# Zero-padded query blocks in one attention, and one PSUM copy with GpSimd adds in the other

## The chip, the core and the metric

The kernel runs on one core of a Trainium2 chip. A core has a matrix engine (TensorE, PE in the rows; its weight loads are listed apart as PEld), VectorE (DVE), ScalarE (ACT), GpSimd (POOL) and SyncE (SP), which issues most DMA transfers. The engines run side by side and wait for one another through semaphores; each takes its instructions in the order of the program. TensorE writes its results into PSUM, from where VectorE and ScalarE take them to SBUF. The metric is the time of one execution on the device, in microseconds (us); smaller is better.

## The reference

Two transformer blocks follow each other, on 1024 tokens of width 1024. Two of their stages matter here.

The first block has an attention with 8 heads of width 64, causal, with a forget gate `c`:

```python
s = jnp.einsum('bqhd,bkhd->bhqk', qb, k) * scale          # 128 queries a block
s = s + cqb[..., :, None] - c_bhs[..., None, :]
s = jnp.where(key_pos[None, :] <= q_pos[:, None], s, -jnp.inf)
p = jax.nn.softmax(s, axis=-1)
out = jnp.einsum('bhqk,bkhd->bqhd', p, v)
```

The second block has an attention with 16 query heads in 4 groups (4 heads share a key head), each block of 128 queries against its own, the previous and the next block of 128 keys and against 256 context keys, with a sink term in the softmax:

```python
s_lat = einsum('bqhgd,bshd->bhgqs', qb, kb) * scale       # up to 384 keys
s_ctx = einsum('bqhgd,bshd->bhgqs', qb, k_ctx) * scale    # 256 keys
p = softmax(concatenate([where(valid, s_lat, -1e30), s_ctx, sink]))
o = p_lat @ vb + p_ctx @ v_ctx
```

Around them stand projections, a gated unit, a feed-forward part, a convolution and a mixture of 16 experts; the change leaves these alone.

## The kernel before

Every fp32 number `x` that enters a matrix product is held as two fp32r numbers, a high part (a ScalarE copy) and a low part `x - high` (a VectorE subtraction), and a product is the sum of two or three products of parts. So PSUM results pass through both ScalarE and VectorE before TensorE uses them again.

**First attention.** The loop `for n in range(N + last + 1)` runs over 64 steps, a step being one head `h` and one block `i` of 128 queries, with `i + 1` blocks of 128 keys. `steps` interleaves the long blocks of a head (i = 7 to 4, score tile `sb` of two banks) with the short ones of the head before (i = 3 to 0, score tile `ss` of one bank), in pairs: two long, two short, and so on. Eight steps make one head's worth of work. Each of `sb` and `ss` has one buffer, so the scores of the second step of a pair wait until VectorE has read the first. The table `ORDB` gives the parts of a step and how many steps each lags behind: S, score products (lag 0); M, VectorE's masked minimum and addition, line 698 (0); E, ScalarE's exponential, line 706 (1); T, the transposition of the probabilities on TensorE, line 721 (3); H and L, high and low part, lines 727 and 731 (3 and 4); V, the product with the values, lines 740 and 741 (6); O, the output out of PSUM, lines 751 to 756 (6); F, the sums and final scale. Within a round the order on every engine is V, L, T, O, F, S, H, M, E.

The score product of 512 keys has two parts and, in the last chunk, the causal mask between them. `q` holds, for the head in question, high and low parts of the query stacked in 128 partitions, `k` the high part of the keys twice; that product (line 685) contracts over 128 partitions. The third product, high part of the query by the low part `l` of the keys, takes the 64 partitions `r` of the head alone (line 688); the other 64 partitions of `l` hold the low part of the other head of the pair.

**Second attention.** 32 units of a head group and a query block, four steps each, run through the table `ORD2` in the same manner, with lags up to 10 for the output (O) and 27 for the final scale (F). A unit takes four score products (lines 1411 to 1414, each over 128 partitions), four VectorE minima (line 1425), four exponentials (1432), five groups of transposes (1444), five high and low parts (1454, 1462) and ten products with the values (1474, 1475), which gather in one PSUM bank `po`, `[128, 512]`: partitions 0 to 63 are the part of the high, 64 to 127 that of the low value parts, columns are four heads by 128 queries. `po` has one buffer. `pv_out2` adds the two halves and puts heads 0 and 2 in partitions 0 to 63 of `og`, heads 1 and 3 in 64 to 127. In 28 of the 32 units (all but the last four) this takes four ScalarE copies out of PSUM (lines 1496 and 1497) and one GpSimd addition (1498). In most units `prep_k` or `prep_q` also stacks keys or queries of the next group, a chain of TensorE, ScalarE and VectorE.

Of the kernel before, what the change touches and what calls it, by code (L numbers as in the profile page):

```python
# [8 lines left out]
F32 = mybir.dt.float32  # L9
F32R = mybir.dt.float32r  # L10
# [3 lines left out]
AF = mybir.ActivationFunctionType  # L14
OP = mybir.AluOpType
# [3 lines left out]
P = 128  # L19
# [3 lines left out]
def fused(tc, x, mix_norm_g, w_in, b_f, sgu_ln_g, sgu_ln_b, w_s, b_s, out_norm_g, w_out,  # L23
# [13 lines left out]
    ACT, DVE, POOL, PE = nc.scalar, nc.vector, nc.gpsimd, nc.tensor  # L37
    act = nc.scalar.activation
    ES = ExitStack()
    L, R = "left", "right"  # L40

    def pool(es, name, bufs=1, side=L, space=None):
        kw = dict(name=name, bufs=bufs)
        if space is not None:
            kw["space"] = space
        else:
            kw["side"] = side
        return es.enter_context(tc.tile_pool(**kw))
# [4 lines left out]
    def rd(ap):  # L53
        return ap.bitcast(F32)

    def split(h, l, src, scale=None):
        if scale is None:
            act(h, src, AF.Copy)  # L58
            DVE.tensor_tensor(l, src, rd(h), op=OP.subtract)  # L59
        else:  # L60
            act(h, src, AF.Copy, scale=scale)
            DVE.scalar_tensor_tensor(l, src, scale, rd(h), op0=OP.mult, op1=OP.subtract)
# [101 lines left out]
    def wsrc(w, k0, kc, c0, n):  # L164
        return w[k0 * P:(k0 + kc) * P, c0:c0 + n].rearrange("(k p) n -> p k n", p=P)
# [151 lines left out]
    for src in (mix_norm_g, out_norm_g, ffn_norm_g, norm1_g_2, norm2_g_2, conv_w_2, b_mod_2, c_2, c_ctx_2):  # L317
        n = 1
# [166 lines left out]
    for g4 in range(2):  # L485
# [3 lines left out]
        o = slice(g4 * 4, g4 * 4 + 4)  # L489
# [84 lines left out]
    qk = []  # L574
# [60 lines left out]
    es_b = ExitStack()  # L635
# [4 lines left out]
    pst = pool(es_b, "pst", 4, space=PSUM)  # L640
    ps1 = pool(es_b, "ps1", 1, space=PSUM)
    pvs = pool(es_b, "pvs", 2, R)
    pol = pool(es_b, "pol", 3, R)
    psm = pool(es_b, "psm", 3, R)
    ppt = pool(es_b, "ppt", 2, R)
    ptn = pool(es_b, "ptn", 2, R)
# [5 lines left out]
    def prep(j):  # L652
        vs[j] = pvs.tile([P, NT, 2, P], F32R, name="vhl")
        h, l = vs[j][:, :, :, :64], vs[j][:, :, :, 64:]
        vv = vraw[:, :, j * P:(j + 1) * P].rearrange("p t (o d) -> p t o d", o=2)
        for o in range(2):
            if 2 * j + o not in cns:
                cn_load(2 * j + o)
        return [
            lambda: act(h, vv, AF.Copy),  # L660
            lambda: DVE.tensor_tensor(l, vv, rd(h), op=OP.subtract),
        ]

    steps = []
# [5 lines left out]
                steps += [(m, 7 - a), (m, 6 - a)]  # L670
    live, half, pts = {}, {}, {}

    def score_mm(n):
        h, i = steps[n]
        q, k, l = qk[h]
        r = slice(64 * (h % 2), 64 * (h % 2) + 64)
        nk = (i + 1) * P
        blk = slice(i * P, i * P + P)
        if i > 3:
            sp = psp.tile([P, T], F32, name="sb", bufs=1)  # L680
        else:
            sp = psp.tile([P, 512], F32, name="ss", bufs=1)
        for c0 in range(0, nk, 512):
            cs = slice(c0, min(c0 + 512, nk))
            PE.matmul(sp[:, cs], q[:, blk], k[:, cs], start=True, stop=False)  # L685
            if c0 + 512 >= nk:
                PE.matmul(sp[:, blk], idR, cmR, start=False, stop=False)
            PE.matmul(sp[:, cs], q[r, blk], l[r, cs], start=False, stop=True)  # L688
        live[n] = sp

    def score_max(n):
# [85 lines left out]
    def done(n, d):  # L777
        h, i = steps[n]
        if i == 0 and h % 2 and h < 7:
            for x, f in zip((FS[0], last + FS[1], last + FS[2], last + FS[3]),  # L780
                            (lambda j: pair_sum(j, 0), lambda j: pair_mul(j, 0), lambda j: pair_sum(j, 1), lambda j: pair_mul(j, 1))):
                if d == x:
                    f(h // 2)
        if (h, i) == (7, 0) and d == dict(ORDB)["E"] + 1:
            DVE.reciprocal(rinv, tns[3][:, 1].rearrange("p i o -> p (i o)"))
            rx[3] = sq.rearrange("p (i o d) -> p i (o d)", o=2, d=64)
            todo.append(lambda: DVE.tensor_copy(rx[3].rearrange("p i (o d) -> p (i o) d", o=2),
                                                rinv[:, :, None].to_broadcast([P, 16, 64])))
# [7 lines left out]
    def stage(f, n):  # L796
        if 0 <= n < N:
            f(n)

    ASQ = max(steps.index((5, 0)) + last + FS[3], steps.index((7, 7))) + 1  # L800
    table = dict(S=score_mm, M=score_max, E=score_exp, T=probs_T, H=probs_H, L=probs_L, V=even(pvmm), O=even(pv_out))
    for n in range(N + last + 1):
        if n < N and steps[n] in ((0, 7), (2, 7), (4, 7), (6, 7)):
            oT.append((pq if oT else po0).tile([P, T], F32, name="qk"))
        for c, d in ORDB:
            if c == "F":
                for d in range(last + 8):
                    stage(lambda m: done(m, d), n - d)
            else:
                stage(table[c], n - d)  # L810
        if n < N and steps[n][1] == 5 and steps[n][0] in (1, 3, 5):
            todo.extend(prep(steps[n][0] // 2 + 1))
        if n < N and steps[n] == (6, 7):

            r4, r5, rw, h4, l4, wh0, wl0 = [pq.tile([P, T], F32 if i < 3 else F32R, name="qk") for i in range(7)]
            k2 = lambda a: a[:, :768].rearrange("p (k n) -> p k n", k=2)
            nc.sync.dma_start(r4, d_sgu[0])
            nc.sync.dma_start(k2(rw), wsrc(w_out, 4, 2, 0, 384))
            nc.sync.dma_start(r5, d_sgu[1])
            todo.extend([lambda: split(h4, l4, r4), lambda: split(k2(wh0), k2(wl0), k2(rw))])  # L820
        if n < N and steps[n] == (7, 7):
            h5, l5, sqs, sq = [pq.tile([P, T], F32R if i < 2 else F32, name="qk") for i in range(4)]
            todo.append(lambda: split(h5, l5, r5))

            def attn_sq(j):
                act(sq if j else sqs, oT[j], AF.Square)
                if j:
                    POOL.tensor_tensor(sqs, sqs, sq, op=OP.add)

            todo.extend([lambda j=j: attn_sq(j) for j in range(2)])  # L830
        if n == ASQ:
            todo.append(lambda: attn_sq(2))
        if todo and n >= 2:
            todo.popleft()()
# [17 lines left out]
    for i in range(NPART):  # L852
        n = -(-(FF - f0) // (NPART - i))
# [53 lines left out]
    for k in (6, 7):  # L907
# [4 lines left out]
                stage=2, scols=1536, pcols=768, name="w2")  # L912
# [48 lines left out]
    vctx = pkc.tile([P, 2, 256], F32, name="vctx")  # L961
# [353 lines left out]
    kst, qst, og, og2, tns, sms, ptt, sps, pos, rx = [{} for _ in range(10)]  # L1315
# [53 lines left out]
    es_b = ExitStack()  # L1369
# [6 lines left out]
    pog = pool(es_b, "pog", 2)  # L1376
# [100 lines left out]
    def pv_out2(n):  # L1477
        u, s = divmod(n, 4)
        if s < 3:
            return  # L1480
        if u % 4 == 0:
            og[u // 4] = pog.tile([P, 2, 512], F32, name="og")
        w = u // 4
        po = pos.pop(u)
        q = slice(u % 4 * P, u % 4 * P + P)
        heads = lambda a: a.rearrange("d (c o q) -> d c o q", o=2, q=P)
        if u % 4 in OD or w == 7:
            lo = pog.tile([64, 512], F32, name="lo")
            act(lo, po[64:], AF.Copy)
            for o in range(2):  # L1490
                DVE.tensor_tensor(og[w][64 * o:64 * o + 64, :, q], heads(po[:64])[:, :, o, :], heads(lo)[:, :, o, :], op=OP.add)
        else:
            lo = pog.tile([P, 2, P], F32, name="lo")
            for o in range(2):
                r = slice(64 * o, 64 * o + 64)
                act(og[w][r, :, q], heads(po[:64])[:, :, o, :], AF.Copy)
                act(lo[r], heads(po[64:])[:, :, o, :], AF.Copy)
            POOL.tensor_tensor(og[w][:, :, q], og[w][:, :, q], lo, op=OP.add)


    def fin_sum(w):
# [52 lines left out]

    todo = deque(prep2(0))
    table = dict(S=score_mm2, M=score_max2, E=score_exp2, T=probs_T2, H=probs_H2, L=probs_L2, V=pvmm2, O=pv_out2, F=fin)
    for n in range(N2 + 40):
        for c, d in ORD2:
# [219 lines left out]
    for r in range(P // 8):  # L1778
        o = slice(8 * r, 8 * r + 8)
# [123 lines left out]
    for t in range(NT + 2):  # L1903
# [9 lines left out]
        u = t - 2  # L1913
        if u >= 0:
            r = rso[:, u:u + 1]
# [66 lines left out]
```

## Time and profile before

| | |
|---|---|
| runs | 3078.14, 3086.30 and 3086.57 us, median 3086.3 us |
| the profiled execution | 3078.3 us, its span 3076.5 us |
| busy share of the span | PE 96%, PEld 79%, DVE 56%, ACT 44%, POOL 11% |
| mean granted TensorE clock | 0.982 of full speed |
| first attention | from about 254 to 415 us of the span |
| second attention | from about 1923 to 2225 us |

The span is the time from the first to the last instruction of the profiled execution; 1.8 us of its time lie outside. Busy shares are averages over all stages. A TensorE that is busy is not a TensorE at its peak: the rows give each product a duration, and how fast products follow each other is read from their starts. Weight loads overlap with the products before them.

### The profile page before, as it was taken

To read this page: it belongs to the slowest core of one execution; us is meant where nothing else is said; L and a number is where in the kernel's file an instruction comes from. 1 tells how busy PE (TensorE), PEld (TensorE's weight loads), DVE (VectorE), ACT (ScalarE), POOL (GpSimd) and SP (SyncE) were. 2 spreads that over 40 slices of the span, in tenths; PEclk is the share of its full clock that TensorE was granted. 3 is DMA by queue.
4 is the path that set the end of the run, shared out by engine and by line. 5 is a ranking of instruction groups with operands and counts; after the bars stand their busy time and mean duration, and the time that the engine had idled before them with its cause. 6 is when DMAs were issued, how large, how long until landed. Compare 5 with 4: busy or idle time off the path is not lost.

```text
span 3076.5 us, 36785 instructions
## 1 busy us (share of the span) xinstructions
PE 2946.9 (96%) x14183; PEld 2442.4 (79%) x14183; DVE 1730.7 (56%) x2485; ACT 1350.4 (44%) x2107; POOL 350.8 (11%) x301
## 2 busy tenths in 40 slices
PE   9999999999999999999999999788899879999996
PEld 7987778888888888788888888677778768888885
DVE  4345763645354445833311123787842479999998
ACT  5345753212111212422121111788821368888886
POOL 2200122000000001200000012111121301111112
PEclk9999999999999999999999999999999889999998
DMA  5120140323222222321122221000153589999997
GB/s 195 44 74 14 40 139 26 108 72 98 67 99 84 92 79 65 126 60 42 55 69 76 89 83 35 1 21 15 44 199 136 178 304 368 377 371 378 377 377 278
DMA packets 287903, 411.88 MB, mean 134 GB/s; under 512 B 13244, under 2 KB 141984, under 8 KB 287728
## 3 DMA queue, kind: packets, MB, share of 16 engines
q1 hardware_dynamic: 275744, 371.34, 34.9%
q0 software_dynamic: 10496, 37.14, 3.9%
q8 instruction: 111, 1.82, 0.3%
q10 hardware_dynamic: 1488, 1.06, 0.2%
q14 instruction: 64, 0.52, 0.1%
HBM read 365.94 MB, written 43.55 MB: 133 GB/s over the span
## 4 chain that ended last, share of the span: by engine, by line
PE 82%; DVE 6%; ACT 5%; issue 3%; DMA 3%; POOL 1%; SPq 0%; POOLq 0%; DVEq 0%; ACTq 0%
PE b L65 24%; PE b L67 24%; PE b L66 24%; ACT sm L1432 1%; ACT ph L1454 1%; PE pt L721 1%; PE b L1823 1%; PE sb L688 1%; PE po L740 1%; DVE wl L59 1%; DVE pl L1462 1%; PE sb L685 1%; PE po L741 1%; DVE sm L1425 1%; PE pt L1444 0%
## 5 line engine op out<-in xcount | busy, mean ns | idle before, releaser
L59 DVE TENSOR_TENSOR wl<-wst,wh 128x1024 fp32r<-128x1024 f32 (+2 forms) x560 | 661.4, 1211 | 452.1 <-ACT wh L58 444.2
L58 ACT ACTIVATE wh<-wst 128x1024 fp32r<-128x1024 f32 (+2 forms) x560 | 578.3, 1044 | 379.7 <-PE b L66 161.1
L66 PE MATMUL b<-xn,wh 128*128 128x512 f32 x1312 | 510.7, 389 | 2.2 <-POOL xn L1185 1.3
L65 PE MATMUL b<-xn,wh 128*128 128x512 f32 x1312 | 511.7, 390 | 0.2 <-ACT xn L1187 0.2
L67 PE MATMUL b<-xn,wl 128*128 128x512 f32 x1312 | 510.8, 389 | 0.5 <-DVE wl L59 0.5
L65 PE MATMUL b<-wh,a 128*128 128x512 f32 x768 | 302.4, 394 | 0.2 <-ACT a L58 0.2
L66 PE MATMUL b<-wl,a 128*128 128x512 f32 x768 | 299.9, 390 | 0.8 <-DVE wl L59 0.8
L67 PE MATMUL b<-wh,a 128*128 128x512 f32 x768 | 299.7, 390 | 0.4 <-DVE a L59 0.4
L66 PEld LDWEIGHTS b<-xn,wh 128*128 128x128 f32 x1312 | 246.4, 188 | 53.8 <-POOL xn L1185 1.7
L67 PEld LDWEIGHTS b<-xn,wl 128*128 128x128 f32 x1312 | 246.3, 188 | 52.3 <-DVE wl L59 1.1
L65 PEld LDWEIGHTS b<-xn,wh 128*128 128x128 f32 x1312 | 246.3, 188 | 51.4 <-ACT xn L1187 0.6
L67 PEld LDWEIGHTS b<-wh,a 128*128 128x128 f32 x768 | 144.6, 188 | 31.0 <-DVE a L59 1.1
L66 PEld LDWEIGHTS b<-wl,a 128*128 128x128 f32 x768 | 144.7, 188 | 30.5 <-DVE wl L59 1.6
L65 PEld LDWEIGHTS b<-wh,a 128*128 128x128 f32 x768 | 144.8, 188 | 29.6 <-ACT a L58 0.7
L65 PE MATMUL b<-hH,wh 128*128 128x512 f32 x352 | 137.7, 391 | 0.0
L67 PE MATMUL b<-hH,wl 128*128 128x512 f32 x352 | 137.1, 389 | 0.0
L66 PE MATMUL b<-hL,wh 128*128 128x512 f32 x352 | 136.9, 389 | 0.0
L1462 DVE TENSOR_TENSOR pl<-pt,ph 128x512 fp32r<-128x512 f32 x152 | 102.1, 687 | 32.5 <-ACT ph L1454 31.5
L1865 POOL DMA_INDIRECT d_x<-b,idxT x15 | 65.8, 4387 | 469.8 <-DVE b L1859 469.8
L58 ACT ACTIVATE hH<-sg 128x512 fp32r<-128x512 f32 x44 | 27.8, 632 | 202.7 <-DVE sg L1049 202.7
L1425 DVE CUSTOM_DVE_ANT_0 sm<-sp,mk,nsk 128x640 f32<-128x640 f32 (+1 forms) x128 | 107.1, 838 | 3.8 <-PE sp L1414 2.4
L1042 ACT ACTIVATE sg<-sg 128x512 f32<-128x512 f32 x44 | 27.7, 633 | 179.6 <-DVE sg L1041 179.6
(511 smaller groups left out, 5501.7 us busy)
## 6 DMA issues: line engine op xcount, KB each, us to landing
wst<-in_w_exp_gate_dram SPq DMA_DIRECT2D x128, 512.0 KB, 10.8
wst<-in_w_exp_up_dram SPq DMA_DIRECT2D x128, 512.0 KB, 10.8
wst<-in_w_exp_down_dram SPq DMA_DIRECT2D x128, 512.0 KB, 11.1
wst<-in_w_in_dram SPq DMA_DIRECT2D x74, 512.0 KB, 3.9
mw<-in_w_mod_dram SPq DMA_DIRECT2D x48, 512.0 KB, 4.8
wst<-in_w_gate_up_dram SPq DMA_DIRECT2D x44, 512.0 KB, 4.1
wst<-in_w_down_dram SPq DMA_DIRECT2D x16, 512.0 KB, 3.8
wst<-in_w_out_dram SPq DMA_DIRECT2D x10, 512.0 KB, 4.0
```

Of the source, the lines that this page charges most:

```text
L58: act(h, src, AF.Copy)
L59: DVE.tensor_tensor(l, src, rd(h), op=OP.subtract)
L65: PE.matmul(ps, lh, rh, start=start, stop=False)
L66: PE.matmul(ps, lh, rl, start=False, stop=False)
L67: PE.matmul(ps, ll, rh, start=False, stop=stop)
L685: PE.matmul(sp[:, cs], q[:, blk], k[:, cs], start=True, stop=False)
L688: PE.matmul(sp[:, cs], q[r, blk], l[r, cs], start=False, stop=True)
L721: PE.transpose(pt[:, b * P:(b + 1) * P], sm[:, (k0 + b) * P:(k0 + b + 1) * P], ident)
L740: PE.matmul(po[:, c:], v, ph[:, kb, c:], start=kb == 0, stop=False)
L1425: DVE.tensor_tensor_reduce(sms[n][:, :nk], sps.pop(n)[:, 256:256 + nk], (mk if i else mk0)[:, :nk], -0.125, nsk[:, hd:hd + 1], op0=OP.add, ...
L1462: DVE.tensor_tensor(pl, pt, rd(ph), op=OP.subtract)
L1865: nc.gpsimd.indirect_dma_start(out=d_x2, out_offset=bass.IndirectOffsetOnAxis(ap=idxT[:, e:e + 1], axis=0), in_=y, in_offset=None, compute ...
```

## The change

In the first attention, GpSimd writes for every step the high part of the query block into one of four tiles `qz` of 128 x 128, whose other 64 partitions were set to zero once; the third score product then takes `qz` and all 128 partitions of `l`. The copy for step n + 2 is put behind the scores of step n. A pool loses a buffer (`pol`, 3 to 2) to make room. In the second attention, `po` leaves PSUM by one ScalarE copy of 128 x 512, and GpSimd moves 64 partitions of it across (into `vctx`, which is no longer needed) and adds, once for each half of the partitions.

```diff
-    pol = pool(es_b, "pol", 3, R)
+    pol = pool(es_b, "pol", 2, R)
...
+    pqz = pool(es_b, "pqz", 1, R)
+    qzs = [[pqz.tile([P, P], F32R, name=f"qz{c}") for c in range(2)], [pqz.tile([P, P], F32R, name=f"qz{2 + c}") for c in range(2)]]
+    for o in range(2):
+        for t in qzs[o]:
+            POOL.memset(rd(t[64 - 64 * o:128 - 64 * o, :]), 0.0)
+    pads = {}
+
+    def pad_q(n):
+        h, i = steps[n]
+        r = slice(64 * (h % 2), 64 * (h % 2) + 64)
+        qz = qzs[h % 2][i % 2]
+        POOL.tensor_copy(qz[r, :], rd(qk[h][0][r, i * P:i * P + P]))
+        pads[n] = qz
+
+    pad_q(0)
+    pad_q(1)
...
-        r = slice(64 * (h % 2), 64 * (h % 2) + 64)
+        qz = pads.pop(n)
...
-            PE.matmul(sp[:, cs], q[r, blk], l[r, cs], start=False, stop=True)
+            PE.matmul(sp[:, cs], qz, l[:, cs], start=False, stop=True)
...
+            if c == "S":
+                stage(pad_q, n + 2)
...
-            lo = pog.tile([P, 2, P], F32, name="lo")
+            both = pog.tile([P, 512], F32, name="lo")
+            act(both, po, AF.Copy)
+            over = vctx[:, u % 2, :].rearrange("p (c q) -> p c q", q=P)
+            hb = heads(both)
             for o in range(2):
-                r = slice(64 * o, 64 * o + 64)
-                act(og[w][r, :, q], heads(po[:64])[:, :, o, :], AF.Copy)
-                act(lo[r], heads(po[64:])[:, :, o, :], AF.Copy)
-            POOL.tensor_tensor(og[w][:, :, q], og[w][:, :, q], lo, op=OP.add)
+                r, x = slice(64 * o, 64 * o + 64), slice(64 - 64 * o, 128 - 64 * o)
+                POOL.tensor_copy(over[r], hb[x, :, o, :])
+                POOL.tensor_tensor(og[w][r, :, q], hb[r, :, o, :], over[r], op=OP.add)
```

TensorE's and VectorE's instructions stand in the same order as before; only the operands of line 688 (706 in the changed kernel) differ. GpSimd's order in the first attention, where `qk` is the stacked output, `ol` the low half and `rx` the spread reciprocals, was:

```order
L568 DMA d_c<-cT 64x128
L756 TENSOR_TENSOR qk<-qk,ol 64x256 x3
L764 COPY rx<-tn 128x256 x2
L756 TENSOR_TENSOR qk<-qk,ol 64x256
L764 COPY rx<-tn 128x256 x2
L756 TENSOR_TENSOR qk<-qk,ol 64x256 x3
```

It is now as follows, from the eleventh padded block on (line 774 of the changed kernel is 756 of the one before):

```order
L685 CAST qz_2061<-qk 64x128
L685 CAST qz_2062<-qk 64x128
L774 TENSOR_TENSOR qk<-qk,ol 64x256
L685 CAST qz_2061<-qk 64x128
L685 CAST qz_2060<-qk 64x128
L685 CAST qz_2059<-qk 64x128
L685 CAST qz_2062<-qk 64x128
L774 TENSOR_TENSOR qk<-qk,ol 64x256
```

The additions, which wait for ScalarE, now have copies behind them on which TensorE's scores wait. ScalarE's order at the first output of the second attention, with the exponentials (`sm`), the high parts (`ph`) and the copies out of `po`, was:

```order
L1432 ACTIVATE sm,tn<-sm,tn 128x640
L1454 ACTIVATE ph<-pt 128x512
L1496 ACTIVATE og<-po 64x2x128
L1497 ACTIVATE lo<-po 64x256
L1496 ACTIVATE og<-po 64x2x128
L1497 ACTIVATE lo<-po 64x256
L1432 ACTIVATE sm,tn<-sm,tn 128x640
L1454 ACTIVATE ph<-pt 128x512 x2
```

It is now:

```order
L1452 ACTIVATE sm,tn<-sm,tn 128x640
L1474 ACTIVATE ph<-pt 128x512
L1514 ACTIVATE lo<-po 128x512
L1452 ACTIVATE sm,tn<-sm,tn 128x640
L1474 ACTIVATE ph<-pt 128x512 x2
```

Three ScalarE instructions fewer stand between one high part and the next exponential.

## Rows read from the trace of the kernel before

**Rows 1.** Starts of line 698 on VectorE, first and last of its 1024-wide form.

```profile
257.99 1.22 DVE L698 CUSTOM_DVE_ANT_0 sb<-sb,wst 128x1024 f32<-128x1024 f32 x1
...
388.95 1.23 DVE L698 CUSTOM_DVE_ANT_0 sb<-sb,wst 128x1024 f32<-128x1024 f32 x1 [0.77 <-PE sb L688]
```

**Rows 2.** Windows: stretch, length, busy PE, PEld, DVE, ACT, POOL, clock, DMA, GB/s.

```profile
296.05:370.50 74.45, 73.84 (x449) 56.61 (x450) 54.74 (x130) 57.01 (x139) 8.80 (x16) 1.00 0.14 49
```

**Rows 3.** Timeline of TensorE: start, duration, line; a long step, first attention.

```profile
303.59 0.48 PE L685 MATMUL sb<-qk 128*128 128x512 f32 x1
304.00 0.50 PE L688 MATMUL sb<-qk 64*128 64x512 f32 x1
304.43 0.39 PE L685 MATMUL sb<-qk 128*128 128x256 f32 x1
304.65 0.22 PE L687 MATMUL sb<-cmR,idR 128*128 128x128 f32 x1
304.80 0.38 PE L688 MATMUL sb<-qk 64*128 64x256 f32 x1
305.11 0.39 PE L740 MATMUL po<-hs,vhl 128*128 128x256 f32 x1
305.33 0.28 PE L741 MATMUL po<-ls,vhl 128*128 128x256 f32 x1
305.45 0.29 PE L740 MATMUL po<-hs,vhl 128*128 128x256 f32 x1
```

**Rows 4.** Timeline of TensorE in a projection, products of 512 columns.

```profile
249.08 0.40 PE L66 MATMUL b<-xtL,wh 128*128 128x512 f32 x1
249.31 0.40 PE L67 MATMUL b<-xtH,wl 128*128 128x512 f32 x1
```

**Rows 5.** Timeline of TensorE, a short step of one key block.

```profile
302.25 0.31 PE L685 MATMUL ss<-qk 128*128 128x128 f32 x1
...
302.85 0.99 PE L721 MATMUL pt<-ident,sb 128*128 128x128 f32 x7
```

**Rows 6.** Timeline, second step of the first attention, with its scores and VectorE's wait.

```profile
259.27 0.49 PE L685 MATMUL sb<-qk 128*128 128x512 f32 x1 [3.13 <-DVE tn L698]
...
261.57 1.09 DVE L698 CUSTOM_DVE_ANT_0 sb<-sb,wst 128x896 f32<-128x896 f32 x1 [2.36 <-PE sb L688]
```

**Rows 7.** GpSimd by line and form, whole span: count, busy, mean ns, idle before.

```profile
L756 POOL TENSOR_TENSOR qk<-qk,ol 64x256 f32<-64x256 f32 x14 | 11.7, 834 | 173.4 <-ACT ol L755 164.0 <-ACT hs L727 9.4
...
L764 POOL COPY rx<-tn 128x256 f32<-128x256 f32 x12 | 4.5, 403 | 8.4 <-DVE tn L761 8.2
...
L611 POOL CAST idR<-ident 128x128 fp32r<-128x128 f32 x1 | 0.3, 301 | 0.0
```

**Rows 8.** Timeline of ScalarE around one output, second attention.

```profile
2032.56 0.57 ACT L1454 ACTIVATE ph<-pt 128x512 fp32r<-128x512 f32 x1
2033.04 0.36 ACT L1496 ACTIVATE og<-po 64x256 f32<-64x256 f32 x1
...
2034.60 0.83 ACT L1432 ACTIVATE sm<-sm,tn 128x640 f32<-128x640 f32 x1
```

**Rows 9.** Windows: one unit with preparation, one without, second attention.

```profile
2033.04:2042.35 9.31, 8.41 (x58) 7.23 (x56) 7.88 (x17) 8.45 (x20) 1.47 (x2) 1.00 0.15 57
...
2090.00:2097.30 7.30, 5.61 (x35) 4.79 (x36) 5.34 (x14) 7.00 (x18) 1.75 (x2) 1.00 0.00 0
```

**Rows 10.** Timeline of TensorE: first value products of two units, with their waits.

```profile
2034.62 0.50 PE L1474 MATMUL po<-ph,vhl 128*128 128x512 f32 x1 [0.74 <-ACT lo L1497]
...
2043.94 0.50 PE L1474 MATMUL po<-ph,vhl 128*128 128x512 f32 x1 [1.75 <-ACT lo L1497]
```

**Rows 11.** Group by line, second attention: count, busy, mean ns, idle before.

```profile
L1474 PE MATMUL po<-ph,vhl 128*128 128x512 f32 x152 | 72.8, 479 | 24.9 <-ACT lo L1497 23.3 <-DVE og L1491 1.4 <-ACT ph L1454 0.2
```

**Rows 12.** Windows: start of the first attention.

```profile
260.00:280.00 20.00, 18.81 (x74) 13.24 (x74) 10.85 (x22) 10.69 (x24) 0.00 (x0) 0.66 0.00 1
```

**Rows 13.** The chain that ended last, just behind the first attention.

```profile
416.20 9.20 DMA wst<-in_w_out_dram
```

## The prediction

> **What bounds the kernel now.** I read the busy times of the two attentions first, then the timeline of the engine that never rests there, then the waits.
>
> In the first attention the eight 1024-wide minima on VectorE start between 257.99 and 388.95 us [rows 1]: seven periods in 130.96 us, 18.7 us a head. Over four of these TensorE is busy for 73.84 of 74.45 us, VectorE for 54.74, ScalarE for 57.01 [rows 2]; per head that is 18.5, 13.7 and 14.3. So TensorE sets the pace, with ScalarE at 77% and VectorE at 74%. The reader should see next that TensorE's business is not column work. In a long step [rows 3] a 512-column product starts at 303.59, the 64-partition one behind it at 304.00 and the next at 304.43: 0.41 and 0.43 us apart, where two 512-column products over 128 partitions start 0.23 us apart [rows 4]. The product that comes after such a one is late as well: from line 740 at 305.11 to 741 it takes 0.22 us, and 0.12 to the next one, both of 256 columns [rows 3]. TensorE neither runs into the 64-partition product nor out of it without a gap.
>
> In the second attention ScalarE sets the pace in most of a unit. Four copies out of `po` stand between 2033.04 and 2034.60, 1.56 us [rows 8], in a unit of 9.31 us in which ScalarE is busy for 8.45, VectorE for 7.88 [rows 9]; what ScalarE lacks is mostly its wait in the preparation of keys. TensorE stops at the first product with the values until the last copy has freed `po`: 0.74 and 1.75 us in two units in a row [rows 10], 23.3 us in all [rows 11].
>
> **First attention: the third product over 128 partitions.** A long step with chunks of 512 and 256 columns takes 1.74 us from 303.59 to 305.33, the following product included [rows 3]. With the spacing of full products, 0.23 for 512 columns [rows 4], 0.12 for 256 and, by half of that, 0.06 for the 128 of the mask [rows 3], the same instructions take 2 x 0.23 + 2 x 0.12 + 0.06 + 0.12 = 0.88. TensorE gains 0.86 us. A short step of one block takes 0.60 us from its first product to the transposes [rows 5]; three products of 128 columns and a start behind transposes, which I leave at the 0.08 us more that it seems to cost, give 0.26, a gain of 0.34. A head has four long steps (two 64-partition products each) and four short ones (one each): 4 x 0.86 + 4 x 0.34 = 4.8 us of TensorE's time, 38 us in 64 steps. TensorE would then need 18.6 - 4.8 = 13.8 us a head.
>
> That is not what the head gains, because ScalarE needs 14.3 and VectorE 13.7 [rows 2]: what is late next is ScalarE, and all three engines are level. The floor is 14.3, a gain of 4.3 at the most. How near three level engines come to their slowest, no row of this stage shows. The nearest is the unit of the second attention, where the slowest engine is busy for 8.45 of 9.31 us, 91%, with the next at 85% [rows 9]; by that the head would take 14.3 / 0.91 = 15.7 us. But the first attention has shorter lags, and its single score buffers tie TensorE and VectorE together within a pair: TensorE cannot score the second step of a pair until VectorE has read the first. I take 88%, 16.2 us, a gain of 2.4 a head, and for the low end 80%, hardly more than ScalarE's 77% now: 17.8 us, a gain of 0.8. Over six heads in the steady part 2.4 makes 14.4 us.
>
> The first head gains differently. There each step waits for the one before: scores of the second step start at 259.27, the minimum on them at 261.57 [rows 6]. TensorE's clock is at 0.66 of full speed there [rows 12], after a wait of 3.13 us [rows 6], so a part of the gaps is twice as long. Two to three tenths of these 2.3 us go; over the eight steps of the head I put 4 us. The last steps behind 388.95 drain, partly paced by VectorE and ScalarE: 1.5 us. First attention: 14.4 + 4 + 1.5 = 20 us.
>
> **What the padding adds.** 64 copies of 64 x 128 on GpSimd and four clears. The nearest rows are a copy of 128 x 128 at 0.30 us and one of 128 x 256 at 0.40 [rows 7]; I take 0.3, 19 us on an engine that is busy for 8.80 of 74.45 [rows 2]. They cost nothing if each is done before its scores are due. The copy for step n + 2 is queued behind the addition of step n - 6, which waits for ScalarE's copies in round n, and in some rounds behind two copies of `rx`. After ScalarE's copies, ScalarE still has the high parts of n - 3 and the exponential of n - 1 to do, on which TensorE's transposes wait that stand ahead of the scores n + 2. That is 1.5 to 2.5 us, against 0.83 + 0.3 for addition and copy [rows 7]. So cover is there; without it, 14 additions and 6 pairs of `rx` would each hold TensorE for up to 1 us, 20 us in all, the whole gain. I take 0 and keep 20 as the bad end. At the start, the first products do not need the padding, and the first minimum on VectorE starts only at 257.99 [rows 1], behind the projection's last results; the clears hide there. The pool with one buffer less holds a tile from ScalarE's copy to the addition behind it, two of which come in eight steps: nothing.
>
> **Second attention: one copy.** A ScalarE instruction of the same size out of PSUM (line 1454) takes 0.48 us from its start to the next [rows 8], so ScalarE gains 1.56 - 0.48 = 1.08 us in each of 28 units, 30 us at the most. `po` is free 1.08 us sooner too, which covers the wait of 0.74 and most of that of 1.75 [rows 10]. What is late next: in the unit with preparation ScalarE would need 9.31 - 1.08 = 8.23 us, VectorE 7.88 [rows 9], TensorE 9.32 - 1.75 = 7.57 (from 2034.62 to 2043.94 without the wait [rows 10]). ScalarE remains the slowest, by little; I take 0.85 of the 1.08. In a unit without preparation (7.30 us [rows 9]) the engines are closer, and I take 0.4. There are 24 preparations, one in a unit; I count 22 of the 28 units with one: 22 x 0.85 + 6 x 0.4 = 21 us. Low end 0.35 a unit, 10 us; high end 28.
>
> GpSimd gets two copies and two additions of 64 x 256 for one addition: about 2 x 0.4 + 2 x 0.73 = 2.3 us a unit (0.83 is the mean of line 756 with two long ones in it [rows 7]), against 8.4. The final scale reads `og` six steps, some 12 us, after the last addition of a window; and the copy of the next unit but one waits for these additions with 16 us to spare. Nothing.
>
> **The sum.** 20 + 21 = 41 us, from the profiled execution's 3078.3 (span 3076.5 and 1.8 around it): 3037.3. The median of the runs is 3086.3, two runs of three lie at 3086, so the profiled execution is an early one; I add half of the 8 us and forecast 3041.
>
> **Rivals.** *Coupling eats it.* Three level engines wait for each other in turn, and ScalarE reaches 80%: 0.8 x 6 + 4 + 1.5 = 10 us in the first attention, 10 in the second: 3078.3 - 20 + 4 = 3062. For it: single buffers of the scores and of `po`, an order laid out for a TensorE that is last. Against it: the unit without preparation goes at ScalarE's pace although VectorE and TensorE are close behind.
>
> *All of it arrives.* 4.3 x 6 + 6 = 32, and 28: 3078.3 - 60 + 4 = 3022. For it: VectorE and ScalarE wait for TensorE now, and the waits should go with it.
>
> *The number of partitions does not matter, and the padding buys nothing.* Then the gaps around the 64-partition products have another cause, such as the sequence of banks, and remain: only the 21 us of the second attention stay, 3078.3 - 21 + 4 = 3061. Against it stands that in rows 3 the gaps stand ahead of and behind just these products. The Trainium skill, TensorE: Matmul & The Clock Gate (Why this matters for your kernels), says that a product over 32 partitions takes the same time as one over 128; by that rule the padding gains 0. The trace disagrees here: 0.43 against 0.23 us. On the other side, the Trainium skill, TensorEngine Tiling (Key Properties), has a change of the tiling mode drain the engine, by which every one of the 96 products over 64 partitions pays twice, as the rows show.
>
> *Slower: the clock.* A TensorE with rests between its products falls to half speed, as from 260 to 280 us after a rest of 3.13 us [rows 6, 12]. The 13.8 us of a head would become 27.6, 11 over the forecast's 16.2. It decides from 41 / 11, so four heads of eight at half speed; with six it would be 3041 + 66 = 3107. Against it: in the second attention TensorE already rests 0.7 to 1.8 us in each unit [rows 10], and the clock of both units stands at 1.00 [rows 9].
>
> *The gain is given back behind the attention.* Right behind the first attention the chain runs through a load of weights for 9.20 us from 416.20 [rows 13]. Did it start at a fixed time, up to 9 us would be lost: 3050. But it is issued once the attention's buffers are free, and moves with its end.
>
> **Chances.** Forecast 0.58 (between 3026 and 3056 with the loss behind the attention), coupling 0.18, all of it 0.13, padding buys nothing 0.06, slower 0.05. The range, 3020 to 3066, takes in the first two rivals and leaves out the tails. A measurement of this kernel tells a change from none at about 0.3%, 9 us. Faster by more than that is nearly all of the first four, 0.93; within it 0.04, for a padding that comes late in every round and a second attention at its low end; slower 0.03, the clock in more than four heads.
>
> **What would show it.** In the changed profile, products of 512 columns start 0.23 us apart on both sides of the third product; the head takes 15.5 to 17 us with ScalarE over 85% busy; waits of the scores are for VectorE, not for GpSimd. In the second attention TensorE's wait at line 1474 falls from 23 us to under 8, and a unit with preparation takes 8.3 to 8.6 us. Wrong would be a TensorE that waits for `qz`, a clock under 0.95 between 280 and 380 us, or VectorE durations that grow while GpSimd adds.

## The result

The changed kernel takes 3027.9 us in the median (3027.3 to 3028.3, four runs) beside 3085.3 for the kernel before (3078.1 to 3086.6, four runs): a ratio of 0.9818, 95% interval 0.9801 to 0.9835. The profiled execution has a span of 3025.5 us at a mean clock of 0.984. The forecast was 3041, in a range from 3020 to 3066. Between the two profiled executions the forecast gain was 41 us and the measured one is 51.0; the rest of the 57 us between the medians is the early profiled execution of before.

Where the gain arises follows from one instruction at a time: its start in the trace after, less its start in the trace before. I worked the shift out from the starts in both traces. It is +1.3 us ahead of the first attention, -23.1 behind it and constant from 440 us on, -21.6 ahead of the second attention (one step of 1.6 at about 1260 us), -49 to -49.9 behind it and -50.7 at the end. So the first attention gains 24.5 us (forecast 20) and the second 28 (forecast 21). The time lies nearer to the rival "all of it arrives" (3022) than to the forecast.

**First attention.** Starts of the 1024-wide minima on VectorE in the changed kernel (start, duration); they answer to [rows 1].

```profile
259.32 1.23 DVE L716 CUSTOM_DVE_ANT_0 sb<-sb,wst 128x1024 f32<-128x1024 f32 x1
275.32 1.22 DVE L716 CUSTOM_DVE_ANT_0 sb<-sb,wst 128x1024 f32<-128x1024 f32 x1
...
367.04 1.22 DVE L716 CUSTOM_DVE_ANT_0 sb<-sb,wst 128x1024 f32<-128x1024 f32 x1
```

The first head takes 16.0 us, the six after it 91.72, 15.3 each. The wait of 0.77 us in front of the minimum [rows 1] is gone. The windows of the changed kernel (stretch, length, busy PE, PEld, DVE, ACT, POOL, clock, DMA, GB/s) are these six heads, two single ones of them, and the start; they answer to [rows 2, 12].

```profile
275.32:367.04 91.72, 89.27 (x678) 83.24 (x677) 82.56 (x196) 83.91 (x209) 27.77 (x68) 1.00 0.13 46
305.70:321.05 15.35, 15.33 (x120) 14.34 (x118) 14.59 (x35) 14.61 (x37) 5.32 (x12) 1.00 0.10 36
321.05:335.77 14.72, 14.16 (x109) 13.21 (x109) 12.44 (x31) 13.16 (x35) 4.41 (x12) 1.00 0.12 37
260.00:280.00 20.00, 17.00 (x92) 14.82 (x93) 12.76 (x27) 13.40 (x28) 2.70 (x9) 0.76 0.00 1
```

TensorE is still busy for 97% of the six heads; ScalarE has gone from 77% [rows 2] to 91%, VectorE from 74% to 90%. Three nearly level engines, and TensorE hardly waits for the others. The heads alternate between 15.35 and 14.72 us; the longer ones hold the transposes of the rescaling. The next view is TensorE's timeline in the changed kernel, a short step and the long step behind it, which answer to [rows 3, 5].

```profile
296.16 0.31 PE L703 MATMUL ss<-qk 128*128 128x128 f32 x1
...
296.53 0.95 PE L739 MATMUL pt<-ident,sb 128*128 128x128 f32 x7
297.23 0.48 PE L703 MATMUL sb<-qk 128*128 128x512 f32 x1
297.55 0.40 PE L706 MATMUL sb<-qk,qz 128*128 128x512 f32 x1
297.78 0.28 PE L703 MATMUL sb<-qk 128*128 128x256 f32 x1
297.90 0.22 PE L705 MATMUL sb<-cmR,idR 128*128 128x128 f32 x1
297.96 0.33 PE L706 MATMUL sb<-qk,qz 128*128 128x256 f32 x1
298.13 0.28 PE L758 MATMUL po<-hs,vhl 128*128 128x256 f32 x1
298.25 0.28 PE L759 MATMUL po<-ls,vhl 128*128 128x256 f32 x1
```

From the first product of the long step to line 759 it is 1.02 us, 1.74 before: 0.72 less. Behind the padded product the next one starts 0.23 later, as between full products [rows 4]. Only the first pair, behind transposes, stands 0.32 apart. The short step takes 0.37 us instead of 0.60. The padding itself, on GpSimd by line and form (count, busy, mean ns, idle before), answers to [rows 7]:

```profile
L685 POOL CAST qz<-qk 64x128 fp32r<-64x128 f32 x64 | 20.7, 334 | 41.5 <-PE sb L706 36.3 <-PE ss L706 3.3
```

GpSimd waits for TensorE; the other way round there is one wait, of 0.9 us before the first padded product.

**Second attention.** ScalarE's timeline around an output in the changed kernel, to be read against [rows 8]:

```profile
2019.59 0.60 ACT L1474 ACTIVATE ph<-pt 128x512 fp32r<-128x512 f32 x1
2020.09 0.59 ACT L1514 ACTIVATE lo<-po 128x512 f32<-128x512 f32 x1
2020.56 0.83 ACT L1452 ACTIVATE sm<-sm,tn 128x640 f32<-128x640 f32 x1
```

From the copy to the exponential it is 0.47 us where four copies took 1.56. The same two units as in [rows 9], one with preparation and one without, from copy to copy in the changed kernel (columns as above):

```profile
2003.72:2011.98 8.26, 8.21 (x58) 7.27 (x56) 7.70 (x17) 7.33 (x18) 2.98 (x5) 1.00 0.17 63
2053.82:2059.90 6.08, 5.44 (x35) 4.82 (x36) 5.34 (x14) 5.88 (x16) 3.28 (x5) 1.00 0.00 0
```

They went from 9.31 to 8.26 us and from 7.30 to 6.08. With preparation VectorE is now the busiest behind TensorE (7.70 of 8.26, ScalarE 7.33); without, ScalarE at 5.88 of 6.08 is still the busiest. From the first copy out of `po` to that of the 29th unit, 28 units went from 254.2 to 225.8 us: 28.4 less, 1.02 a unit.

Not all of this is ScalarE's time. Three of the 28 units ran at a lower granted clock in the kernel before, and at full clock in the changed one. The rows are one of them before and after, and the same kind of unit in `pad_only` (below), whose second attention is the old one, once at the lower and once at full clock:

```profile
2080.29:2090.00 9.71, 8.32 (x45) 7.03 (x43) 7.32 (x16) 7.78 (x19) 0.74 (x1) 0.82 0.01 3
...
2046.51:2053.82 7.31, 6.73 (x45) 5.63 (x43) 6.96 (x16) 6.54 (x16) 2.26 (x4) 1.00 0.02 3
...
1985.15:1994.85 9.70, 8.30 (x45) 7.04 (x43) 7.36 (x16) 7.78 (x19) 0.73 (x1) 0.82 0.01 2
2060.66:2068.78 8.12, 6.74 (x45) 5.69 (x43) 7.14 (x16) 7.52 (x19) 0.74 (x1) 1.00 0.02 4
```

With the same instructions the clock costs 9.70 - 8.12 = 1.58 us, so by my estimate 3 x 1.58 = 4.7 of the 28.4 us came from the clock and 23.7 from the copies. (A fourth unit at 0.85 before is matched by one at 0.83 after.) In the unit of the first row TensorE had rested 0.50 and then 1.31 us, the latter for `po`, before the clock fell. It rested as long in both units of `pad_only`, and there the clock fell in one and not in the other, so the cause of the fall stays open. Groups by line of the changed kernel in the second attention (count, busy, mean ns, idle before and its releasers), the first of which answers to [rows 11]:

```profile
L1494 PE MATMUL po<-ph,vhl 128*128 128x512 f32 x152 | 71.3, 469 | 7.5 <-ACT lo L1514 6.0 <-DVE og L1511 1.3 <-ACT ph L1474 0.2
...
L1520 POOL TENSOR_TENSOR og<-lo,vctx 64x256 f32<-64x256 f32 x56 | 41.2, 735 | 4.5
...
L1519 POOL COPY vctx<-lo 64x256 f32<-64x256 f32 x56 | 22.0, 393 | 111.0 <-ACT lo L1514 109.5
...
L1367 ACT ACTIVATE qs<-pt 64x512 fp32r<-64x512 f32 x30 | 17.7, 591 | 52.2 <-PE pt L1363 37.9 <-DVE qs L1368 14.3
```

TensorE's wait for `po` went from 23.3 us to 6.0. ScalarE now waits 14.3 us for VectorE in the preparation of queries.

### The profile page after: what moved, and what is told of

The parts are those of the page before. It is cut to its first block, busy times and chain, and to the rows that moved or that the text cites. A ratio compares the mean times of both kernels' runs of the same rounds, so it can differ in the third digit from the quotient of the medians.

```text
span 3025.5 us, 36880 instructions
## 1 busy us (share of the span) xinstructions
PE 2910.0 (96%) x14183; PEld 2435.0 (80%) x14183; DVE 1726.5 (57%) x2485; ACT 1318.9 (44%) x2023; POOL 413.1 (14%) x453
## 3 DMA queue, kind: packets, MB, share of 16 engines
q10 hardware_dynamic: 1488, 1.06, 0.2%
## 4 chain that ended last, share of the span: by engine, by line
PE 85%; DVE 5%; ACT 4%; issue 2%; DMA 2%; POOL 1%; SPq 0%; POOLq 0%; ACTq 0%; DVEq 0%
PE b L65 25%; PE b L67 25%; PE b L66 25%; PE pt L1464 1%; PE b L1845 1%; PE po L1494 1%; PE po L1495 1%; DVE wl L59 1%; DVE pl L1482 1%; PE b L1725 1%; DVE sm L1445 1%; PE pt L739 1%; DVE qs L1368 1%; PE b L1687 0%; DMA ot<-d_o 0%
```

## The experiments

Theory: in the first attention the price is TensorE's change between products over 128 and over 64 partitions; in the second it is ScalarE's time. Rivals: banks or something else in the order of the products; the time at which `po` is released; ScalarE as the new bound of the first attention; GpSimd's work as a cost. A shift is always that of the same instructions against the trace named.

**The two parts alone.** `pad_only` is the changed kernel with the old `pv_out2`, `copy_only` the kernel before with the new one.

> Padded query blocks alone, the second attention as before. Theory (the two parts act on stages that lie far apart and add up): the first attention is shorter by 24 to 25 us as in the changed kernel, a unit of the second attention takes 9.3 us again; 3052 to 3056 us, or up to 3060 if what lifts the runs of the kernel before from 3078 to 3086 us sits in the second attention. Rival (a part of the gain in the first attention hangs on the second part, or is given back behind it): a different shift behind the first attention than 24.5 us.

> The single copy out of PSUM alone, the first attention as before. Theory: the second attention is shorter by 27 to 28 us, a head of the first takes 18.7 us again; 3050 to 3058 us. Rival (as above, not additive): clearly less than 27 us in the second attention.

`pad_only` took 3054.3 us (ratio 0.9904, 0.9887 to 0.9920), `copy_only` 3050.7 (0.9893, 0.9877 to 0.9910), beside 3082.1. In the traces the first loses 24.5 us in the first attention and nothing in the second, the other one nothing in the first and 29.8 in the same 28 units of the second, all of them at full clock. The parts add up but for 1.4 us, about what one unit of the changed kernel lost at a granted clock of 0.83 (10.12 us, against 8.57 of a like one).

**Padding kept, its use undone.** The clears and GpSimd's copies stay; the third product takes the 64 partitions that hold the query.

```diff
-            PE.matmul(sp[:, cs], qz, l[:, cs], start=False, stop=True)
+            PE.matmul(sp[:, cs], qz[r], l[r, cs], start=False, stop=True)
```

> The changed kernel, all of GpSimd's copies kept, but the third score product takes only the 64 partitions of the head out of the padded tile. Theory (the gain comes from the product's 64 partitions alone): gaps of 0.2 us on both sides return, a head takes 18.7 us, the time rises by 24 to 25 us to 3052. Rival 1 (the gain comes from the other weight tile, or from GpSimd's copy itself): stays at 3028. Rival 2 (the copies have a price that the padding hides): above 3055.

It took 3053.9 us (0.9906, 0.9889 to 0.9922); the steady heads of the first attention are back at their old 18.3 and 18.9 us (the whole is 1.4 us shorter than before, 1.1 of it in the first head), the second keeps its 28. TensorE's timeline of this kernel in a long step:

```profile
302.91 0.47 PE L704 MATMUL sb<-qk 128*128 128x512 f32 x1
303.32 0.50 PE L707 MATMUL sb<-qk,qz 64*128 64x512 f32 x1
303.75 0.39 PE L704 MATMUL sb<-qk 128*128 128x256 f32 x1
```

The gaps of 0.41 and 0.43 us are those of [rows 3]. Same operands in the same tile, same banks, same order: the number of partitions alone brings them.

**Fewer changes, no padding.** In the kernel before, both 64-partition products of a long step go to its end.

```diff
                 PE.matmul(sp[:, blk], idR, cmR, start=False, stop=False)
+        for c0 in range(0, nk, 512):
+            cs = slice(c0, min(c0 + 512, nk))
             PE.matmul(sp[:, cs], q[r, blk], l[r, cs], start=False, stop=True)
```

> The kernel before with one edit: in a long step both products over 64 partitions stand at the end, next to each other, so that there are 64 changes into them and out instead of 96; their number, size and order of sums per bank are kept. Theory (the price is paid at a change between 128 and 64 partitions, about 0.4 us for in and out): 32 changes fewer, TensorE gains 32 x 0.43 = 14 us, a head takes 17 us; 3064 to 3072 us. Rival (each 64-partition product is slow by itself): no change, 3078 to 3086 us, and the two neighbours start 0.43 us apart.

It took 3069.8 us (0.9955, 0.9938 to 0.9972), 11 us less in the first attention. The long step in this kernel's timeline of TensorE:

```profile
302.07 0.59 PE L685 MATMUL sb<-qk 128*128 128x512 f32 x2
302.50 0.22 PE L687 MATMUL sb<-cmR,idR 128*128 128x128 f32 x1
302.65 0.61 PE L690 MATMUL sb<-qk 64*128 64x512 f32 x2
303.19 0.39 PE L742 MATMUL po<-hs,vhl 128*128 128x256 f32 x1
303.42 0.28 PE L743 MATMUL po<-ls,vhl 128*128 128x256 f32 x1
```

1.35 us, 0.39 less than [rows 3] with two changes fewer: 0.2 for a change, the mean of both ways. In the starts behind the merged row the two neighbours are 0.33 us apart, not 0.43 as by the rival. So most of the price is the change's, not that of each 64-partition product. The Trainium skill, TensorEngine Tiling (Array Packing) (Key Properties), says that switching the mode requires a drain; the runs agree and put 0.2 us to it.

**GpSimd's copies.** 60 of the 64 query copies are left out, so that most steps score with the wrong query block.

```diff
-        POOL.tensor_copy(qz[r, :], rd(qk[h][0][r, i * P:i * P + P]))
+        if (h % 2, i % 2) not in seen:
+            POOL.tensor_copy(qz[r, :], rd(qk[h][0][r, i * P:i * P + P]))
+            seen.add((h % 2, i % 2))
```

> The changed kernel with 60 of the 64 copies of query blocks left out: each of the four padded tiles is filled once, and most scores are then taken with the wrong low term. Theory (the copies lie beside other work, but for the start): 3025 to 3028, TensorE's 2 us of waits for the first blocks stay. Rival (GpSimd's queue holds the scores, or its traffic slows VectorE): 5 to 15 us less.

3027.8 us (0.9822, 0.9805 to 0.9838), the changed kernel's time: the copies cost nothing that can be measured.

**Is ScalarE the bound of the first attention now?** In `one_copy_both` the outputs of heads 0 to 6 leave `po` by one ScalarE copy too, and GpSimd moves and adds.

```diff
-            act(dst, po[:64], AF.Copy)
-            act(ol[r], po[64:], AF.Copy)
+            act(ol, po, AF.Copy)
+            POOL.tensor_copy(dst, ol[x])
             POOL.tensor_tensor(dst, dst, ol[r], op=OP.add)
```

> The changed kernel with the same idea in the first attention: for heads 0 to 6 every output leaves PSUM by one ScalarE copy of 128 x 256, GpSimd moves 64 partitions across into the result and adds; this takes one ScalarE copy of 0.38 us from 14 outputs and a VectorE addition of 0.42 us from 14 others. Theory (with the gaps gone ScalarE is the slowest there, busy for 55.6 of 60.2 us in four heads, VectorE next): 3 to 7 us less, 3021 to 3025. Rival (GpSimd's longer queue makes the padded blocks late): 3028 or more, with TensorE waiting for them.

3027.9 us (0.9821, 0.9804 to 0.9837): no gain. The same two heads as above, from minimum to minimum in this kernel:

```profile
305.29:320.60 15.31, 15.29 (x119) 14.29 (x118) 13.86 (x32) 13.70 (x35) 8.59 (x18) 1.00 0.11 36
320.60:335.32 14.72, 14.17 (x109) 13.21 (x109) 11.61 (x29) 12.26 (x33) 7.50 (x18) 1.00 0.10 37
```

ScalarE does 0.9 us less in a head, VectorE 0.7 to 0.8, and the heads take as long to 0.04 us. TensorE's 15.29 and 14.17 us are nearly unchanged. VectorE's waits for TensorE's scores grow from 9.1 to 19.2 us; TensorE's products wait 1.6 us for `qz`, 0.9 in the changed kernel, so the rival's late blocks explain 0.7 us at the most. ScalarE isn't the bound.

**Is it TensorE?** `no_mask` leaves the causal mask's product out, so that the softmax takes in later keys.

```diff
-            if c0 + 512 >= nk:
-                PE.matmul(sp[:, blk], idR, cmR, start=False, stop=False)
```

> The changed kernel without the causal mask's product in the first attention (64 products of 128 columns; its softmax then takes in later keys too). The run with one copy in both attentions took 3 to 4 us each off ScalarE and VectorE there and gained nothing. Theory now (TensorE is still the one that sets the pace of a head, busy for 97% of it, not ScalarE as predicted): 64 x 0.06 to 0.11 = 4 to 7 us less in the first attention, 3021 to 3025. Rival (as predicted, ScalarE or the coupling of all three paces): at most 1 us less, 3027 to 3028.

3026.9 us (3022.5 to 3030.6; 0.9819, 0.9801 to 0.9837): the times are too far apart to tell. In the trace the first attention is 2.9 us shorter, less than the theory's 4 and more than the rival's 1. A head with rescaling and one without, from minimum to minimum in this kernel:

```profile
303.51:318.86 15.35, 15.14 (x112) 13.32 (x110) 14.60 (x36) 14.62 (x38) 5.32 (x12) 1.00 0.09 36
318.86:332.80 13.94, 13.32 (x101) 12.25 (x101) 12.25 (x32) 12.98 (x34) 4.36 (x12) 1.00 0.10 39
```

The heads without rescaling go from 14.72 to 13.94 us, so TensorE is their bound. Those with it stay at 15.35, whether some of ScalarE's and VectorE's work is taken away or the mask. What holds these stays open.

**ScalarE's time in the second attention.** Behind the one copy, three copies of 64 x 256 of SBUF onto itself load ScalarE as before, while `po` is released early.

```diff
             act(both, po, AF.Copy)
+            for _ in range(3):
+                act(both[:64, :256], both[:64, :256], AF.Copy)
```

> The changed kernel, and behind its one copy out of PSUM ScalarE copies a quarter of the result (64 x 256) three times onto itself, in SBUF: po is free as soon as in the changed kernel, ScalarE has about its old load of 1.5 us a unit again. Theory (ScalarE's time sets the pace of a unit): a unit takes 9.1 to 9.4 us again, 20 to 28 us come back, 3048 to 3056. Rival (the gain is that TensorE gets po sooner): at most 8 us come back, 3028 to 3036.

3054.2 us (0.9905, 0.9889 to 0.9922): the 28 units take 251.4 us, so 25.6 of the 28.4 are gone again. The load is a little above the old one: the first unit of [rows 9] takes 9.46 us, 9.32 before. VectorE's low parts in this kernel wait for ScalarE's high parts, as in the kernel before (32.5 us, 31.5 of it for `ph`); in the changed kernel they wait 8.4 us, 7.8 of it for `ph`:

```profile
L1482 DVE TENSOR_TENSOR pl<-pt,ph 128x512 fp32r<-128x512 f32 x140 | 94.3, 687 | 34.4 <-ACT ph L1474 34.0
```

**The release of `po`.** In `late_free` a ScalarE instruction that reads one column of `po` follows behind the next exponential, and GpSimd's adds with it; `small_only` is the same, but it reads the copy in SBUF.

```diff
+            act(both[:, 0:1], po[:, 0:1], AF.Copy)
```

```diff
-            act(both[:, 0:1], po[:, 0:1], AF.Copy)
+            act(both[:, 0:1], both[:, 0:1], AF.Copy)
```

> The changed kernel, but ScalarE reads one more column of po behind the next exponential, so that po is free about 1 us later, about when the last of the old four copies freed it; ScalarE gets one small instruction more, some 0.2 us a unit (GpSimd's additions come behind it too). Theory (ScalarE's time sets the pace): 2 to 6 us come back, 3030 to 3034. Rival (TensorE getting po sooner is the gain): 15 to 25 us come back, 3043 to 3053, with TensorE's wait at the first value product at 20 us and more.

> The run late_free with one edit: the small ScalarE instruction behind the next exponential reads the copied tile in SBUF instead of po, so po is free early again, and all else (the instruction, GpSimd's additions behind it) stays. Theory (of late_free's 11 us the later release of po is the larger part, since TensorE waited 20 us for it): 2 to 4 us above the changed kernel, 3030 to 3032. Rival (the small instruction itself, and what is queued behind it, costs the 11 us): 3036 to 3040.

`late_free` took 3039.2 us (0.9858, 0.9842 to 0.9874), which is what neither expected; its second attention is 14 us longer. In `small_only` that is -1 us, at 3025.1 (0.9814, 0.9798 to 0.9831), below the 3030 to 3032 expected, so the 14 are the release and not the instruction. TensorE in `late_free`:

```profile
L1494 PE MATMUL po<-ph,vhl 128*128 128x512 f32 x148 | 69.7, 471 | 20.6 <-ACT lo L1525 19.9 <-DVE og L1511 0.4 <-ACT ph L1474 0.2
```

That is nearly the 23.3 us of [rows 11]. So my theory was half of it: the late release alone costs 14 of the 28 us, and ScalarE's load alone 25.6. They overlap, and either is enough to lose half of the gain or more.

**What the waits point to.** In the preparation ScalarE copies the first half, VectorE subtracts, and ScalarE's second copy out of the same tile waits for it. In `acts_first` both copies come first, in `prep_k` and in `prep_q` (shown).

```diff
             act(q[0:64, cs], pt[64 * o:64 * o + 64], AF.Copy)
+        for o in range(2):
+            q = qst[g, 2 * pr + o]
             DVE.tensor_tensor(q[64:128, cs], pt[64 * o:64 * o + 64], rd(q[0:64, cs]), op=OP.subtract)
```

> The changed kernel with one more edit in the second attention's preparation: both ScalarE copies of a group of keys or queries stand ahead of the VectorE subtractions, where now the second copy waits for the first subtraction (14.3 and 7.4 us of waits of ScalarE in all). Theory (ScalarE paces the units with preparation): 5 to 15 us less, 3013 to 3023. Rival 1 (VectorE, busy nearly as long, takes the wait over): 3025 to 3028. Rival 2 (the transposes' bank is held longer, TensorE waits): 3028 or more.

3018.1 us (3017.0 to 3020.1; 0.9796, 0.9780 to 0.9812): all its runs lie below all of the changed kernel's, by 7 us at least, though the two were not timed side by side. In the trace the second attention is 10.5 us shorter than the changed kernel's. Its waits in the preparation:

```profile
L1370 DVE TENSOR_TENSOR qs<-pt,qs 64x512 fp32r<-64x512 f32 x30 | 20.7, 689 | 9.4 <-ACT qs L1367 9.1
L1367 ACT ACTIVATE qs<-pt 64x512 fp32r<-64x512 f32 x28 | 16.6, 593 | 6.9 <-PE pt L1363 6.7
```

ScalarE's 14.3 us behind VectorE are gone. This is the fastest version of all.

## Why the prediction was right, and where not

- **The gaps around the 64-partition products: right.** `half_padded` brings them back, `grouped64` takes about half of them away. The rival of a padding that buys nothing is refuted, and with it, for products among full ones, the rule that the prediction cites from the Trainium skill, TensorE: Matmul & The Clock Gate (Why this matters for your kernels), that a product over 32 partitions takes as long as one over 128. No run here shows such a product alone.
- **TensorE's gain of 4.8 us a head: 1.0 too large.** The long step gained 0.72 (forecast 0.86), the short one 0.23 (0.34): 4 x 0.72 + 4 x 0.23 = 3.8. I took 0.23 and 0.12 us for all products; those behind transposes still start 0.32 apart, and the last padded one is followed after 0.17.
- **"What is late next is ScalarE", and 88% of coupling: failed.** Since TensorE gained less, it is busy for 14.9 us a head and stays the slowest; `one_copy_both` shows that ScalarE isn't, and `no_mask` that TensorE is in every other head. And the slowest engine loses 3%, not 12%: the head takes 15.3 us, not 16.2. The two errors had opposite signs, so that the 20 us came near the 24.5 by luck. The 91% of the second attention was a poor stand-in: 0.7 of the 0.86 us that ScalarE lacks in that unit are its wait for VectorE in the preparation, the kind of wait that `acts_first` removes. The prediction also read VectorE's 85% as the next engine there, where [rows 9] have TensorE at 8.41 of 9.31, 90%.
- **First head 4 us, tail 1.5: the first too large.** It went from 18.8 us (257.99 to 276.76 before) to 16.0, 2.8 less, and the clock from 0.66 to 0.76. Tail: 24.5 - 20.5 - 2.8 = 1.2.
- **The padding at no cost: right** (`few_pads`). TensorE waited for `qz` once, 0.9 us at the start (the weight load of that product 1.3).
- **One copy, 0.85 and 0.4 us a unit: too small.** The 1.56 became 0.47, as forecast, and units with preparation take 8.5 us in the mean of seven, as forecast (8.3 to 8.6). But 28.4 us in 28 units are 1.02 of the 1.09. The unit without preparation was the term mis-sized most: 1.22 instead of 0.4, since no engine came up against ScalarE there. I had VectorE come up against it with preparation; at 7.70 of 8.26 it did, and the unit still gained 1.06. And some 4.7 of the 28.4 us are the clock's in three units (estimated above), which the forecast had at nothing. GpSimd's work showed no price: VectorE's low parts take 685 ns beside it, 687 before.
- **Given back behind the attention: refuted.** The shift is constant from 440 us on.
- **Slower by the clock: refuted, and the other way round in part.** The six heads stand at 1.00. Against this rival the prediction held that the clock stands at 1.00 in both units of [rows 9], in spite of TensorE's rests. [rows 9] are no others than these two: in three other units the kernel before had it at 0.82, and the changed kernel did not.

## What to carry to other kernels

Read how far apart products start, not how long the trace says they last: one over 64 partitions among full ones costs a change on each side, and zeros in the other half, written by an idle engine, take both away. An engine that is level with two others can still be busy for 97% of the time, as TensorE was here; look for the wait, not for a rule of thumb. Compare the same units before and after, and read the granted clock of each. When one copy replaces four, the time of the engine and the release of the PSUM buffer both count, and here the next gain lay where that engine waited in the middle of a pair of copies.

## What the runs showed of the hardware

A change of TensorE between 128 and 64 partitions took about 0.2 us in the mean of both ways. Four ScalarE copies of 64 x 256 out of PSUM took 1.56 us, one of 128 x 512 with the same data 0.47. Moving 64 partitions across cost GpSimd 0.39 us for 256 columns. Between two traces of this kernel there are jumps of some 1.6 us at a few places, and those looked at are stretches of lower granted clock that one trace has and the other lacks. The step at about 1260 us is one: from 1235.4 to 1239.0 us of the changed kernel's trace the clock is at 0.53 (the lower of its two levels is 0.50), and at the same work in the kernel before, 1258.5 to 1262.1 us, at 1.00. TensorE was busy in both, with products of one column ahead of it. Whether such stretches are also what spreads the times of `no_mask` over 8 us is not shown.
